# First products computed ahead of the feed-forward loop: for ten up sets of ten column pairs in place of the gate and up sets of five

## The chip, the cores and the metric

The kernel runs on one core of a Trainium2 chip. Its metric is the time of one execution in device microseconds (us). The kernel before took 1977.85 us as the median of three runs (1973.35 to 1978.29).

## The reference, cut to what matters

One decoder layer over 520 tokens (512 of a prompt, 8 samples, and 16 meta tokens that end before this stage). After attention and pooling come two layer norms with a feed-forward block between them. The change lies at the first of these two norms and in the gate and up products behind it:

```
h1 = layer_norm(DEEPNORM_ALPHA * h + mix, ln1_g, ln1_b)
a = jax.nn.silu(jnp.einsum('btd,df->btf', h1, w_gate)) * jnp.einsum('btd,df->btf', h1, w_up)
ff = jnp.einsum('btf,fd->btd', a, w_down)
return layer_norm(DEEPNORM_ALPHA * h1 + ff, ln2_g, ln2_b)
```

`h1` has 2048 columns, `w_gate` and `w_up` are 2048 x 5632, all in fp32.

## The kernel before, in words

**Tiling.** The 5632 hidden columns are 44 tiles of 128, taken as 22 column pairs (tile i and tile i + 22). For each pair there is one `Set` for the gate weights and one for the up weights (class at L924). A set multiplies a 2 x 2 block of weights by a 2 x 2 block of activations with seven products in place of eight (Winograd's form of Strassen's scheme): products 1 to 7, `Set.prod` at L941. The two halves of the tokens are 260 columns each, `HN`.

**One product.** Its weight block is 128 x 1024 fp32, in two halves of 512. Each half is split (L181) into a high part, a cast on ScalarE (ACT, L185), and a low part, a subtraction on VectorE (DVE, L186); then TensorE (PE) runs 12 matmuls on it (L201, L202, L204), so 24 for a product. The split halves live in a ring of five buffers (`WB`). Products 7, 6, 5 and 3 need a sum or difference of weight blocks first, made in place on VectorE by `weight_sum` (L191; it is recorded under L194). The sum for 7 overwrites block (1,0) from (0,0) and (1,0); for 6 it overwrites (1,0) from (1,1) and (1,0); for 5 it overwrites (0,0) from (1,0) and (0,0); for 3 it overwrites (0,1) from (0,1) and (1,0). So the sum for product 7 is the first sum of a set, and it wants blocks (0,0) and (1,0) in place; the sum for product 3 is the last reader of (1,0), and the splits of product 5 are the last readers of (0,0).

**Loads.** `load_raw` (L175) brings a 512 KB weight block in through SP's DMA queue (the issue is L178) into a ring of five buffers (`NRAW`). A set loads four blocks, in the order in which `run` asks for them. A load must wait until the block five loads before it in the ring has had its last reader. SP's queue also carries the staging stores of 260 KB to `t_d` (L1057, L1064).

**A set that runs in full** asks for (0,0), (1,0), (1,1), (0,1). It computes product 1, copies it out on ScalarE (L985), then products 7, 6, 2, 5, 4, 3, with two more copies on ScalarE (L995, L1001).

**Products ahead.** While the second half's layer norm is computed, TensorE would have nothing to do. Half of the tokens is normalised by then, so product 1, whose activations are block (1,1) of that half, can already be computed: `Set.ahead` (L958) does it with plain fp32 matmuls (L963) straight from the loaded weights. For the first two sets, the gate and up set of pair 0 (`NKEEP`), products 1 and 2 stay in PSUM. For the next ten sets (`NFILL`) product 1 is copied to SBUF by ScalarE (L968) into the `fill` tiles. `step` (L158) writes these matmuls' order on TensorE by hand.

**A filled set**, one with its first product ahead, runs six products: 7, 6, 2, 5, 4, 3. In place of the three copies on ScalarE it adds the stored product on VectorE three times (L993, L999, L1015). It asks for its blocks in the order (1,0), (0,0), (1,1), (0,1), since product 7 now comes first.

**Around it.** `turn` lists the pairs; the loop at L1095 runs `gate_out` and then `up_out` for each, with the staging of the pair before (`staged`, L1041: sums, casts and stores to `t_d`) as side steps within the gate set. Pairs are numbered here in the order of `turn`, from 0. On VectorE, ScalarE, SP and, outside the steps, on TensorE a planner orders the instructions by its own estimates of costs; each engine then runs its list in order.

Of the kernel before, what the change touches and what calls it, by code (L numbers as in the profile page):

```python
# [37 lines left out]
NFILL = 10  # L38
NF = 5
NKEEP = 2  # L40
# [26 lines left out]
def hybrid_step(ctx, tc, xin, w_in, w_o, w_g, w_u, w_d, w_pool, par_d, cst_d, ident_d, ln2gb, kct_d, vc_d, hist_d,  # L67
# [746 lines left out]
    for h in range(2):  # L814
        for k2 in range(KT // 2):
            mh[h].append(slot(f"mh{h}_{k2}"))
            ml[h].append(slot(f"ml{h}_{k2}"))
            for kk in range(2):
                s = mixf[2 * k2 + kk][:, HALF[h]]
# [255 lines left out]
    sets = [Set(w, i, f"{n}{i}") for i in turn for n, w in (("g", w_g), ("u", w_u))]  # L1075
    g1 = ln1(1, zs1)
    fills = [s.ahead(n) for n in (1, 2) for s in sets[:NKEEP]]
    for j, s in enumerate(sets[NKEEP:NKEEP + NFILL]):
        if j % 2 == 0:
            f = pb.tile([P, 2, HN], F32, tag="fill", name=f"fill{j}", bufs=NF)  # L1080
        fills.append(s.ahead(1, f[:, j % 2, :]))
# [314 lines left out]
```

## Time and profile before

| | |
|---|---|
| median of three runs | 1977.85 us (1973.35 to 1978.29) |
| the profiled execution's own time | 1976.38 us |
| its span, first to last instruction | 1974.6 us |
| TensorE busy | 1916.5 us, 97% |
| VectorE busy | 1545.2 us, 78% |
| ScalarE busy | 936.6 us, 47% |
| mean granted TensorE clock | 0.987 |

A busy share is an average over stages. In the gate and up stage (602 to 1490 us) the reader should look at single pairs: how long a pair takes, how many matmuls fall into it, and which wait ended last before an engine went on. A matmul's own duration (0.28 us) is longer than its distance from the next one, since matmuls overlap; counts of matmuls in a stretch tell more than busy time.

### The profile page before, as it was taken

What the parts mean: (1) busy time and instruction counts of PE and PEld (TensorE: products, weight loads), DVE (VectorE), ACT (ScalarE), POOL (GpSimd) and SP (SyncE); (2) the same over time, 40 slices, a digit from 0 to 9 for tenths busy, and PEclk for the clock granted to TensorE, in tenths of its full rate; (3) what the DMA queues carried; (4) which work ended last, traced back from release to release, by engine and by line L of the source; (5) the groups of instructions that cost most, each with busy time, mean ns of one, the idle gap of its engine ahead of it and who ended that gap; (6) DMA issues with size and microseconds to landing.
All of it is one profiled execution on the core that took longest, in us unless ns stands there. A gap on an engine that the chain in (4) does not pass through costs nothing.

```text
span 1974.6 us, 39350 instructions
## 1 busy us (share of the span) xinstructions
PE 1916.5 (97%) x15571; PEld 1881.8 (95%) x15571; DVE 1545.2 (78%) x2730; ACT 936.6 (47%) x1805; POOL 2.5 (0%) x8
## 2 busy tenths in 40 slices
PE   8999999999999999999999999999999999999995
PEld 8999999999988888999999999999999999999995
DVE  6665657766776878788888888888777888888878
ACT  6644445545654434455554545555545434344331
POOL 0000000000000000000000000000000000000000
PEclk9999999999999999999999999999999999999997
DMA  8732222665744453545445453545549664645332
GB/s 264 231 101 67 67 81 71 216 201 170 247 151 145 136 174 125 171 136 167 145 140 162 148 169 125 169 143 169 176 173 365 209 223 166 223 168 202 86 97 87
DMA packets 144984, 319.25 MB, mean 162 GB/s; under 512 B 14160, under 2 KB 65944, under 8 KB 144696
## 3 DMA queue, kind: packets, MB, share of 16 engines
q1 hardware_dynamic: 143680, 314.65, 48.2%
q8 instruction: 122, 2.00, 0.4%
q10 hardware_dynamic: 1120, 2.10, 0.3%
q14 instruction: 62, 0.51, 0.1%
HBM read 265.20 MB, written 54.03 MB: 162 GB/s over the span
## 4 chain that ended last, share of the span: by engine, by line
PE 58%; DVE 5%; DMA 2%; issue 1%; ACT 1%; DVEq 0%; ACTq 0%; SPq 0%
PE tri L201 7%; PE tri L204 7%; PE tri L202 7%; PE p_u L201 6%; PE p_u L202 6%; PE p_u L204 6%; PE p_g L201 6%; PE p_g L204 6%; PE p_g L202 6%; DMA fr<-in_w_g_dram 2%; DVE fr L194 2%; DVE rr L186 1%; PE d L204 1%; DMA t_d<-fr 1%; PE d L202 1%
## 5 line engine op out<-in xcount | busy, mean ns | idle before, releaser
L185 ACT CAST rr<-fr 128x512 fp32r<-128x512 f32 (+1 forms) x1056 | 655.6, 643 | 849.7 <-DVE fr L194 289.0
L186 DVE TENSOR_TENSOR rr<-fr,rr 128x512 fp32r<-128x512 f32 (+1 forms) x1056 | 733.4, 716 | 265.6 <-ACT rr L185 253.7
L194 DVE TENSOR_TENSOR fr<-fr 128x1024 f32<-128x1024 f32 (+1 forms) x304 | 319.3, 1050 | 37.3 <-DMA fr<-in_w_g_dram 21.7
L201 PE MATMUL p_g<-rr 128*128 128x260 f32 x800 | 231.2, 290 | 15.9 <-DVE fr L999 6.7
L204 PE MATMUL p_g<-rr 128*128 128x260 f32 x800 | 225.8, 287 | 1.1 <-DVE rr L186 1.1
L201 PE MATMUL p_u<-rr 128*128 128x260 f32 x800 | 225.5, 283 | 0.0
L204 PE MATMUL p_u<-rr 128*128 128x260 f32 x800 | 222.0, 282 | 0.0
L202 PE MATMUL p_g<-rr 128*128 128x260 f32 x768 | 219.6, 287 | 0.0
L202 PE MATMUL p_u<-rr 128*128 128x260 f32 x768 | 216.0, 282 | 0.0
L204 PE MATMUL tri<-rr 128*128 128x260 f32 x696 | 196.8, 283 | 1.2 <-DVE rr L186 1.2
L201 PE MATMUL tri<-rr 128*128 128x260 f32 x696 | 197.1, 283 | 0.8 <-ACT rr L185 0.8
L202 PE MATMUL tri<-rr 128*128 128x260 f32 x696 | 196.7, 283 | 0.0
L201 PEld LDWEIGHTS p_g<-rr 128*128 128x128 f32 x800 | 154.2, 193 | 19.9 <-DVE fr L999 7.7
L204 PEld LDWEIGHTS p_g<-rr 128*128 128x128 f32 x800 | 153.3, 193 | 1.4 <-DVE rr L186 1.3
L201 PEld LDWEIGHTS p_u<-rr 128*128 128x128 f32 x800 | 150.6, 188 | 0.0
L204 PEld LDWEIGHTS p_u<-rr 128*128 128x128 f32 x800 | 149.7, 189 | 0.0
L202 PEld LDWEIGHTS p_g<-rr 128*128 128x128 f32 x768 | 148.0, 193 | 0.0
L201 PE MATMUL o<-rr 128*128 128x260 f32 x512 | 146.0, 286 | 0.3 <-ACT rr L185 0.3
L202 PEld LDWEIGHTS p_u<-rr 128*128 128x128 f32 x768 | 144.3, 188 | 0.0
L204 PE MATMUL o<-rr 128*128 128x260 f32 x512 | 143.9, 283 | 0.2 <-DVE rr L186 0.2
L202 PE MATMUL o<-rr 128*128 128x260 f32 x512 | 144.0, 282 | 0.0
L204 PEld LDWEIGHTS tri<-rr 128*128 128x128 f32 x696 | 131.3, 189 | 1.7 <-DVE rr L186 1.4
(299 smaller groups left out, 4591.5 us busy)
## 6 DMA issues: line engine op xcount, KB each, us to landing
fr<-in_w_g_dram SPq DMA_DIRECT2D x95, 512.0 KB
fr<-in_w_u_dram SPq DMA_DIRECT2D x95, 512.0 KB
fr<-in_w_d_dram SPq DMA_DIRECT2D x64, 640.0 KB
t_d<-fr SPq DMA_DIRECT2D x140, 260.0 KB
fr<-in_w_o_dram SPq DMA_DIRECT2D x64, 512.0 KB
fr<-in_w_in_dram SPq DMA_DIRECT2D x46, 512.0 KB
rr<-t_d SPq DMA_DIRECT2D x87, 260.0 KB
mid_b<-t_d SPq DMA_DIRECT2D x53, 260.0 KB
```

The lines of the kernel that those rows point to most:

```text
L185: nc.scalar.copy(wh, s)
L186: last_lo[0] = (lo or nc.vector).tensor_sub(wl, s, wh.bitcast(F32)).ins
L194: i = op(*args).ins
L201: nc.tensor.matmul(o, wh, hi[j], start=first, stop=False, skip_group_check=onto)
L202: nc.tensor.matmul(o, wh, lo[j], start=False, stop=False, skip_group_check=onto)
L204: nc.tensor.matmul(o, wl, hi[j], start=False, stop=last, skip_group_check=onto)
```

## The change

One line changes, the choice of the ten sets whose product 1 is computed ahead:

```diff
     fills = [s.ahead(n) for n in (1, 2) for s in sets[:NKEEP]]
-    for j, s in enumerate(sets[NKEEP:NKEEP + NFILL]):
+    for j, s in enumerate(sets[NKEEP + 1::2][:NFILL]):
         if j % 2 == 0:
             f = pb.tile([P, 2, HN], F32, tag="fill", name=f"fill{j}", bufs=NF)
         fills.append(s.ahead(1, f[:, j % 2, :]))
```

`sets` alternates gate and up. Before, `sets[2:12]` are the gate and up sets of pairs 1 to 5. After, `sets[3::2][:10]` are the up sets of pairs 1 to 10. So the gate sets of pairs 1 to 5 run in full, and the up sets of pairs 6 to 10 become filled ones. The code of a set, which isn't changed, then goes one way or the other:

```python
            if not filled:
                self.p1 = r[:, HALF[0]]
                if al is None:
                    al = bank(f"p1_{self.name}")
                    self.prod(1, al)
                nc.scalar.copy(self.p1, al)
            else:
                al = bank(f"p1_{self.name}")
            ga = bank(f"p7_{self.name}")
            next(side, None)
            self.prod(7, ga)
```

## Rows read from the trace of the kernel before

**Rows 1.** The page: the span, and the busy time, share and instructions of each engine.

```profile
span 1974.6 us, 39350 instructions
PE 1916.5 (97%) x15571; PEld 1881.8 (95%) x15571; DVE 1545.2 (78%) x2730; ACT 936.6 (47%) x1805; POOL 2.5 (0%) x8
```

**Rows 2.** Busy time by stretch, one row for each of the pairs 1 to 10: stretch and its length in us, busy us (and instructions) of TensorE's matmuls, its weight loads, VectorE, ScalarE and GpSimd, then the granted TensorE clock, the DMA share and GB/s. A stretch begins where the up set of the pair before does its last multiplication on VectorE.

```profile
637.10:682.30 45.20, 40.71 (x326) 39.46 (x327) 38.03 (x63) 19.86 (x37) 0.00 (x0) 1.00 0.44 147
682.30:723.60 41.30, 37.53 (x290) 36.28 (x289) 33.35 (x56) 16.99 (x31) 0.00 (x0) 0.96 0.46 148
723.60:764.80 41.20, 37.45 (x290) 36.40 (x290) 33.45 (x57) 17.22 (x32) 0.00 (x0) 0.96 0.46 148
764.80:805.70 40.90, 37.65 (x290) 36.40 (x289) 33.31 (x56) 17.13 (x31) 0.00 (x0) 0.96 0.47 149
805.70:844.60 38.90, 36.90 (x293) 36.49 (x292) 32.24 (x55) 16.95 (x31) 0.00 (x0) 0.96 0.46 151
844.60:882.60 38.00, 36.66 (x301) 36.03 (x301) 32.54 (x53) 20.26 (x39) 0.00 (x0) 1.00 0.47 153
882.60:922.80 40.20, 40.20 (x338) 40.20 (x337) 34.30 (x54) 21.41 (x41) 0.00 (x0) 1.00 0.47 152
922.80:963.10 40.30, 40.30 (x338) 40.30 (x338) 34.34 (x54) 21.07 (x41) 0.00 (x0) 1.00 0.45 152
963.10:1003.40 40.30, 40.30 (x338) 40.30 (x337) 34.39 (x54) 21.21 (x41) 0.00 (x0) 1.00 0.45 151
1003.40:1043.70 40.30, 40.30 (x338) 40.30 (x337) 34.39 (x54) 21.43 (x41) 0.00 (x0) 1.00 0.48 152
```

**Rows 3.** Who waited for whom: what TensorE waited for from 640 to 885 us, and what VectorE's weight sums waited for from 640 to 850 us (us in total, times, longest).

```profile
PE p_g L201 <- ACT rr L185: 7.4, 10, 1.7
PE p_g L201 <- DVE fr L999: 6.7, 5, 1.4
...
DVE fr L194 <- DMA fr<-in_w_g_dram: 16.2, 5, 4.1
```

**Rows 4.** The chain of waits that ended last, 660 to 845 us, its five waits for a load of gate weights: start (the issue), us from there to the landing.

```profile
668.29 6.03 DMA fr<-in_w_g_dram
...
709.86 5.85 DMA fr<-in_w_g_dram
...
750.13 6.79 DMA fr<-in_w_g_dram
...
791.96 5.90 DMA fr<-in_w_g_dram
...
832.22 6.88 DMA fr<-in_w_g_dram
```

**Rows 5.** VectorE in order of time, from the filled up set of pair 5 through pair 6 (both sets in full): start, us, line, shape, count, and in brackets the idle time before it and what ended it. L194 is a weight sum, L186 the low part of a split.

```profile
820.00 1.28 DVE L186 TENSOR_TENSOR rr<-fr,rr 128x512 fp32r<-128x512 f32 x2
...
830.98 1.22 DVE L194 TENSOR_TENSOR fr<-fr 128x1024 f32<-128x1024 f32 x1
...
839.13 1.23 DVE L194 TENSOR_TENSOR fr<-fr 128x1024 f32<-128x1024 f32 x1 [2.33 <-DMA fr<-in_w_g_dram]
...
852.95 1.88 DVE L186 TENSOR_TENSOR rr<-fr,rr 128x512 fp32r<-128x512 f32 x3
...
860.01 1.23 DVE L194 TENSOR_TENSOR fr<-fr 128x1024 f32<-128x1024 f32 x1 [0.92 <-DMA fr<-in_w_u_dram]
...
861.98 1.29 DVE L186 TENSOR_TENSOR rr<-fr,rr 128x512 fp32r<-128x512 f32 x2 [0.41 <-ACT rr L185]
```

**Rows 6.** The same for single instructions elsewhere: the first weight sum of pair 1's gate set; in pair 8 the first sum of the up set with the splits behind it; the first sum of pair 9's and of pair 11's gate set.

```profile
634.47 1.23 DVE L194 TENSOR_TENSOR fr<-fr 128x1024 f32<-128x1024 f32 x1 [0.36 <-DMA fr<-in_w_g_dram]
...
940.91 1.22 DVE L194 TENSOR_TENSOR fr<-fr 128x1024 f32<-128x1024 f32 x1 [1.24 <-DMA fr<-in_w_u_dram]
...
942.87 1.29 DVE L186 TENSOR_TENSOR rr<-fr,rr 128x512 fp32r<-128x512 f32 x2 [0.40 <-ACT rr L185]
...
959.72 1.22 DVE L194 TENSOR_TENSOR fr<-fr 128x1024 f32<-128x1024 f32 x1
...
1040.30 1.22 DVE L194 TENSOR_TENSOR fr<-fr 128x1024 f32<-128x1024 f32 x1
```

**Rows 7.** SP's queue in order of time: loads issued behind the sums and splits that free their buffers, in the up set of pair 5 and in the gate sets of pairs 6 and 8 (x2 and x3: so many issues in a row, from that start).

```profile
829.28 3.27 SPq L178 DMA_DIRECT2D fr<-in_w_g_dram  x3
...
854.26 0.95 SPq L178 DMA_DIRECT2D fr<-in_w_u_dram  x2
...
934.24 0.95 SPq L178 DMA_DIRECT2D fr<-in_w_u_dram  x2
```

**Rows 8.** TensorE in order of time: the first matmul of the up set of pair 6 and of pair 8.

```profile
861.92 0.28 PE L201 MATMUL p_u<-rr 128*128 128x260 f32 x1
...
942.50 0.28 PE L201 MATMUL p_u<-rr 128*128 128x260 f32 x1
```

**Rows 9.** Groups of instructions by line, shapes apart: busy us in all, mean ns of one, idle time before them.

```profile
L186 DVE TENSOR_TENSOR rr<-fr,rr 128x512 fp32r<-128x512 f32 x264 | 174.0, 686 | 37.0 <-ACT rr L185 36.1 <-PE p_u L204 0.4
L1006 DVE TENSOR_TENSOR fr<-p_u,fr 128x260 f32<-128x260 f32 x10 | 4.2, 421 | 0.0
...
L963 PE MATMUL p_g<-fr 128*128 128x260 f32 x112 | 25.9, 382 | 0.0
L963 PE MATMUL p_u<-fr 128*128 128x260 f32 x112 | 25.7, 382 | 0.0
```

## The prediction, made before the changed kernel was run

> **What bounds the kernel now.** I read the page first. TensorE is busy 97% of the span, VectorE 78% [rows 1], so the whole kernel looks bound by TensorE. The second view, busy time by pair, says where that isn't so [rows 2]. Pairs 7 to 10, with all sets run in full, take 40.3 us for 338 matmuls and TensorE never pauses: 40.3 / 338 = 0.1192 us a matmul. Pairs 2 to 4, with both sets filled, have 48 matmuls fewer and still take about as long, 40.9 to 41.3 us. At 0.1192 a matmul the losses of pairs 1 to 6 (length less instructions times 0.1192) are 6.3, 6.7, 6.6, 6.3, 4.0 and 2.1, together 32.1 us. So the ten products ahead buy nothing here: TensorE saves 5.7 us a pair and then waits longer than that. The granted clock is a part of these losses: a mean of 0.96 in pairs 2 to 5, that is 2.4 GHz with some time at 1.2 GHz after TensorE's waits, and 1.00 behind.
>
> Third, who waited for whom [rows 3]: TensorE waits for splits on ScalarE and for VectorE's add at L999, and VectorE in turn for loads of gate weights, 16.2 us in five waits. Fourth, the chain of waits has these five loads with 5.85 to 6.88 us from issue to landing [rows 4]. So in filled pairs a loop of VectorE's work and loads sets the pace, not TensorE: the load is issued when the last reader of an older block in the ring of five is done, it lands six us later, and only then can VectorE's next sum begin. The question is how long this loop is after the change.
>
> **What the change removes and adds.** Five gate sets (pairs 1 to 5) go from filled to full, five up sets (pairs 6 to 10) the other way. A full set has one product more: two casts, two subtractions of 0.69 us, 24 matmuls and three copies on ScalarE, where a filled set has three adds of 0.42 us on VectorE [rows 9]. Five such trades in each direction: the sum over the kernel is zero on every engine. The ten products ahead are the same matmuls, 0.38 us each for both kinds of weights [rows 9], of the same 512 KB loads, at the same place: no cost and no gain, hidden or not. What moves is the pair's balance: pairs 1 to 10 each have one full gate set and one filled up set, 312 matmuls, 312 x 0.1192 = 37.2 us of TensorE. VectorE's work of a pair is about that of pairs 7 to 10, 34.3 us [rows 2].
>
> **The new loop, step by step.** In which buffers of the ring the blocks fall follows from five buffers and four loads a set. A full gate set loads (0,0), (1,0), (1,1), (0,1), the filled up set behind it (1,0), (0,0), (1,1), (0,1). Five loads back from the up set's (0,0) is the gate's (0,0), whose last reader is the split for product 5. Five loads back from the next gate's (1,0) is the up set's (1,0), whose last reader is the sum for product 3. Both loads are wanted by the first sum of their set. VectorE takes its list in order, so while that sum waits, nothing behind it starts: the splits of product 7, and with them all that TensorE is to get.
>
> Four terms make the loop.
> - A: from the first sum of a gate set to the issue of the up set's (0,0). The trace has this very transition, a full gate set behind a filled up set, in pair 6: the sum begins at 839.13 [rows 5], the load goes out at 854.26 [rows 7]: 15.13 us.
> - B: that load's landing. In pair 6 the next sum starts at 860.01, 5.75 us from the issue; in pair 8 at 940.91, from 934.24, 6.67 us [rows 5 to 7]. In both VectorE was waiting for the load, so these are landings. I take 6.21, their mean.
> - C: the filled up set, from its first sum to the issue of the load that its sum for product 3 frees. From the sum to the first split 1.96 us (940.91 to 942.87) [rows 6]; from the first split to that issue, in the up set of pair 5, 820.00 to 832.22, 12.22 us [rows 4, 5]; less one add of the gate set (L1015), 0.42, which a full gate set doesn't have [rows 9]. 13.76 us.
> - D: the landing of the next gate's (1,0). It is the third load in a row behind a filled up set [rows 7], as the five of the chain are: their mean is 6.29 us [rows 4].
>
> A + B + C + D = 15.13 + 6.21 + 13.76 + 6.29 = 41.4 us, more than TensorE's 37.2. So each of the ten pairs takes about 41.4 us, and TensorE waits some 4 us in it: 0.75 at the up set, where it arrives at 861.92 [rows 8] and product 7's first split is over only at 861.98 + 0.69 [rows 5], the rest in the gate set, where pair 6 lost 2.1 us [rows 2]. Product 1 of the up set covered the first of these, and covers it no more.
>
> From the first sum of pair 1's gate set (634.47) to that of pair 11 (1040.30) the kernel before takes 405.8 us [rows 6]; after, 10 x 41.4 = 414. Up to 634.47 nothing differs, and from pair 11 on both run full sets. The difference is 8.2 us. On the profiled execution's own 1976.38 us that is 1984.6; the median of the runs shown lies 1.5 above that execution, so 1986. Ends: B from 5.75 to 6.67 and D from 5.85 to 6.88 give loops of 40.5 to 42.4, 1977 to 1996.
>
> At B and D a rule speaks for a better end. The Trainium skill, DMA: Bandwidth & Descriptors, section Anatomy of one DMA, gives a transfer (on its GpSimd path) some 2.0 us fixed and its bytes at 436 GB/s. For 512 KB that is an estimate of 3.2 us, twice in the loop 6.4, and the loop would be 35.3 us, under TensorE's. The five waits of the chain show 5.85 to 6.88 us for such a load with others in the queue [rows 4], and by them the sum goes.
>
> **Rivals.** *TensorE sets the pace after all.* If A shrinks, as the planner may put pair 6's staging steps and multiplications behind the splits of product 5, or the landings are short, the loop falls under 38 us. It decides below 37.2: then ten pairs take 372 us, 34 less, 1944; with 3 us out of the loop, 38.4, it is 384, 22 less, 1956. For it: pairs 7 to 10 run without a pause at 85% of VectorE. Against: their planned order has been repeated in every pair, and pair 6, the only pair of the needed kind, lost time. The figure of the Trainium skill for a transfer (DMA: Bandwidth & Descriptors, Anatomy of one DMA) would lead here too.
>
> *It evens out.* With the landings at their low ends the loop is 40.5 us, hardly other than 40.6, the mean before (405.8 / 10): 1977 to 1980. For it: the third load's spread is wide [rows 4]. Against: in that case both landings must be low in all pairs.
>
> *Worse.* Each load shares SP's queue with the staging stores; at the high ends, 6.67 and 6.88, and with 0.5 us of a store's issue ahead of each, the loop is 43.4: 434 us, 28 more, 2006. It decides from 42.5 on. For it: landings of 6.79 and 6.88 stand in two of five waits. Against: they aren't the mean. A clock that falls in each pair, as in pairs 2 to 5, costs little by itself while VectorE's loop is the longer one: TensorE has 4 us to spare in it.
>
> **How the numbers follow.** 0.3% is 5.9 us, about what a measurement of this kernel can tell from no change. Chances: the loop of 41.4 and its neighbourhood (1979 to 1996) 0.52, of which 0.38 lies over 5.9 and 0.14 within; evening out 0.23, all within; TensorE's pace 0.17, all faster; worse 0.08. So faster 0.17, same 0.37, slower 0.46. The likeliest case's own range is 1977 to 1996. The range that should hold the time 8 times in 10 leaves out the ends of the two outer rivals: 1960 to 1996.
>
> **What would show it.** In the trace of the changed kernel: the first sum of a gate set recurs every 41.4 us in pairs 1 to 10; VectorE idles before it (2 to 3 us) for gate weights and before the up set's first sum (3 us) for up weights; L999 no longer holds TensorE in gate sets; the stretch of each of the ten pairs has about 314 matmuls and 41 us. TensorE without a pause in pairs 2 to 10 and sums 37 to 38 us apart would prove the first rival. If the sum of the up set stands at some other place in VectorE's order, or if (0,0) goes out before the split of product 5, the terms A and C are wrong and with them the sign.

## The result, and the profile after

The kernel after takes 1959.08 us (median of six runs, 1956.14 to 1960.61), beside 1975.98 us for six runs of the kernel before. The ratio is 0.9915, with a 95% interval of 0.9904 to 0.9927: faster by 0.85%. The forecast was 1986 us, slower, with a range of 1960 to 1996; the direction is wrong, and the time lies just below the range. The execution whose profile follows took 1960.28 us.

First the page of the kernel after (span, then busy time and instructions by engine), to be held against [rows 1]:

```profile
span 1958.5 us, 39300 instructions
PE 1909.2 (97%) x15571; PEld 1875.7 (96%) x15571; DVE 1542.9 (79%) x2730; ACT 937.9 (48%) x1805; POOL 2.5 (0%) x8
```

Every engine has as many of these instructions as before (the total of the first line also counts waits and issues), so the work is the same. The span is 16.1 us shorter. TensorE is busy for 7.3 us less, so 8.8 us of its waiting went, and 7.3 us in which the same matmuls ran more slowly.

Where it went, the second view says: busy time by pair of the kernel after, pairs 1 to 11, columns as in [rows 2] (the tenth row is pair 10, the last with a filled set).

```profile
636.40:678.10 41.70, 40.10 (x328) 39.27 (x327) 35.73 (x58) 19.51 (x37) 0.00 (x0) 1.00 0.46 154
678.10:717.50 39.40, 38.15 (x314) 37.53 (x313) 33.54 (x55) 19.31 (x36) 0.00 (x0) 1.00 0.46 155
717.50:755.60 38.10, 37.81 (x315) 37.52 (x314) 33.59 (x55) 19.31 (x36) 0.00 (x0) 1.00 0.48 160
755.60:794.90 39.30, 38.29 (x315) 37.67 (x314) 33.67 (x56) 19.31 (x36) 0.00 (x0) 1.00 0.47 156
794.90:832.80 37.90, 37.62 (x314) 37.41 (x313) 33.55 (x55) 19.30 (x36) 0.00 (x0) 1.00 0.47 161
832.80:871.30 38.50, 37.99 (x314) 37.57 (x314) 33.60 (x55) 19.30 (x36) 0.00 (x0) 1.00 0.49 159
871.30:911.00 39.70, 38.19 (x314) 37.57 (x313) 33.60 (x56) 19.30 (x36) 0.00 (x0) 1.00 0.47 154
911.00:950.50 39.50, 38.21 (x314) 37.58 (x313) 33.59 (x56) 19.30 (x36) 0.00 (x0) 1.00 0.47 155
950.50:989.60 39.10, 38.20 (x314) 37.57 (x313) 33.59 (x56) 19.30 (x36) 0.00 (x0) 1.00 0.47 156
989.60:1029.60 40.00, 38.17 (x314) 37.55 (x313) 33.56 (x56) 19.30 (x36) 0.00 (x0) 1.00 0.45 152
1029.60:1067.80 38.20, 38.20 (x320) 38.20 (x319) 32.57 (x52) 21.34 (x41) 0.00 (x0) 1.00 0.47 151
```

Pairs 1 to 10 together last 393.2 us and have 3156 matmuls. At 0.1192 us each these would be 376.2, so 17.0 us are lost: 10.5 in which TensorE isn't busy (393.2 less the 382.73 of the busy column), and 6.5 in which matmuls follow each other more slowly. The same sums over pairs 1 to 6 of [rows 2] give 18.6 and 13.5, the 32.1 us of the prediction. The loss was halved: 8.1 us of pauses went and 7.0 of slow matmuls. The granted clock is 1.00 in every row, where four rows of before have 0.96. The missing 0.04 of those four rows' 162.3 us is 6.5 us, about all of the slow matmuls that went.

Who still waits, in the kernel after from 640 to 1030 us (us in total, times, longest), beside [rows 3]:

```profile
PE p_u L201 <- ACT rr L185: 5.8, 7, 1.3
PE p_u L201 <- DVE fr L999: 2.9, 10, 0.3
PE p_u L204 <- DVE rr L186: 1.8, 8, 0.2
...
DVE fr L194 <- DMA fr<-in_w_u_dram: 34.4, 10, 4.3
```

All of TensorE's waits are now in the up sets (`p_u`), none in the gate sets. VectorE's weight sums wait for up weights, once in each of ten pairs, and no longer for gate weights. VectorE can afford most of that: of its 34.4 us TensorE's pauses show no more than the 10.5 that the three rows add up to, 5.8 of them for the casts behind such a sum.

VectorE in order of time, pair 4 of the kernel after: the first sum of the gate set, of the up set, then the sums for products 6, 5 and 3 of the up set, and the first sum of pair 5's gate set (columns as in [rows 5]).

```profile
750.15 1.22 DVE L194 TENSOR_TENSOR fr<-fr 128x1024 f32<-128x1024 f32 x1
...
771.88 1.22 DVE L194 TENSOR_TENSOR fr<-fr 128x1024 f32<-128x1024 f32 x1 [3.53 <-DMA fr<-in_w_u_dram]
...
775.19 1.22 DVE L194 TENSOR_TENSOR fr<-fr 128x1024 f32<-128x1024 f32 x1
...
778.91 1.22 DVE L194 TENSOR_TENSOR fr<-fr 128x1024 f32<-128x1024 f32 x1
...
780.99 1.22 DVE L194 TENSOR_TENSOR fr<-fr 128x1024 f32<-128x1024 f32 x1
...
789.37 1.22 DVE L194 TENSOR_TENSOR fr<-fr 128x1024 f32<-128x1024 f32 x1
```

And SP's queue there: the issue of the up set's (0,0) in pair 4, and that of the next gate set's (1,0).

```profile
765.56 0.35 SPq L178 DMA_DIRECT2D fr<-in_w_u_dram  x1
...
782.27 0.33 SPq L178 DMA_DIRECT2D fr<-in_w_g_dram  x1
```

The four terms of the forecast can be read here. A: 750.15 to 765.56, 15.41 us (forecast 15.13). B: 765.56 to 771.88, 6.32; the mean over the ten pairs is 6.23 (forecast 6.21). C: 771.88 to 782.27, 10.39, not 13.76. D: the load of 782.27 lands 3.84 us later (by its semaphore in the trace), first of its three and not third, and the gate set's sum at 789.37 doesn't wait for it. Gate sets' first sums stand 39.0 us apart on average (633.78 in pair 1 to 1024.11 in pair 11, ten pairs), not 41.4.

C is short because of VectorE's list. In the filled up sets of the kernel before, the planner put all four splits of products 5 and 4 ahead of the sum for product 3. After the change it puts one split of product 4 and then that sum straight behind the sum for product 5: 778.91 to 780.99 in the rows above. That sum frees the buffer of (1,0).

### The profile page after: what moved, and what is told of

Same layout as the page of the kernel before. It is cut to its first block, busy times and chain, and to the rows that moved or that the text cites. A ratio compares the mean times of both kernels' runs of the same rounds, so it can differ in the third digit from the quotient of the medians.

```text
span 1958.5 us, 39300 instructions
## 1 busy us (share of the span) xinstructions
PE 1909.2 (97%) x15571; PEld 1875.7 (96%) x15571; DVE 1542.9 (79%) x2730; ACT 937.9 (48%) x1805; POOL 2.5 (0%) x8
## 5 line engine op out<-in xcount | busy, mean ns | idle before, releaser
L186 DVE TENSOR_TENSOR rr<-fr,rr 128x512 fp32r<-128x512 f32 (+1 forms) x1056 | 733.1, 715 | 246.1 <-ACT rr L185 234.2
L194 DVE TENSOR_TENSOR fr<-fr 128x1024 f32<-128x1024 f32 (+1 forms) x304 | 319.3, 1050 | 50.9 <-DMA fr<-in_w_u_dram 44.4
L201 PE MATMUL p_g<-rr 128*128 128x260 f32 x830 | 233.9, 283 | 2.2 <-DVE fr L1009 2.2
L204 PE MATMUL p_g<-rr 128*128 128x260 f32 x830 | 230.8, 282 | 0.0
L201 PE MATMUL p_u<-rr 128*128 128x260 f32 x770 | 218.4, 284 | 2.9 <-DVE fr L999 2.9
L202 PE MATMUL p_g<-rr 128*128 128x260 f32 x788 | 221.2, 282 | 0.0
L204 PE MATMUL p_u<-rr 128*128 128x260 f32 x770 | 213.6, 282 | 0.0
L202 PE MATMUL p_u<-rr 128*128 128x260 f32 x748 | 210.7, 282 | 0.0
L201 PEld LDWEIGHTS p_u<-rr 128*128 128x128 f32 x770 | 144.9, 188 | 5.0 <-DVE fr L999 5.0
L204 PEld LDWEIGHTS p_u<-rr 128*128 128x128 f32 x770 | 143.9, 189 | 0.0
L202 PEld LDWEIGHTS p_u<-rr 128*128 128x128 f32 x748 | 140.6, 188 | 0.0
```

Source lines behind the costliest of these rows:

```text
L186: last_lo[0] = (lo or nc.vector).tensor_sub(wl, s, wh.bitcast(F32)).ins
L194: i = op(*args).ins
L201: nc.tensor.matmul(o, wh, hi[j], start=first, stop=False, skip_group_check=onto)
L202: nc.tensor.matmul(o, wh, lo[j], start=False, stop=False, skip_group_check=onto)
L204: nc.tensor.matmul(o, wl, hi[j], start=False, stop=last, skip_group_check=onto)
```

## The experiments

### Was it the place of one sum?

My first theory was this order: an early sum for product 3, so an early load, so no wait at the gate set. The rival said that loads don't matter and one filled set in each pair merely balances VectorE's work. A second rival was the clock, whose falls went. `e1_late_sum` puts the splits back in front of the sum, by chaining the low parts of a filled up set one behind the other (the sum is chained to the last of them in any case, L191):

```diff
...
-            last_lo[0] = (lo or nc.vector).tensor_sub(wl, s, wh.bitcast(F32)).ins
+            prev, last_lo[0] = last_lo[0], (lo or nc.vector).tensor_sub(wl, s, wh.bitcast(F32)).ins
+            if chain[0]: tc.add_manual_dep(last_lo[0], prev.name, mybir.DependencyInfo(mybir.DependencyClass.NoSync, mybir.DependencyReason.DATA), reason="low")
...
+            chain[0] = filled and self.name[0] == "u"
             self.prod(5, al, False)
...
```

> The changed kernel, with one thing put back: in the filled up sets VectorE does the four splits of products 5 and 4 ahead of the sum for product 3, as it did in the up sets of the kernel before. No work is added. Order theory (the early sum lets the next gate set's (1,0) be asked for 3.4 us sooner and first in line, and that is what my forecast missed): the loop of my forecast closes again, 40.5 to 41.4 us a pair for 39.0, 15 to 24 us more, 1974 to 1983; the gate set's first sum waits for its weights again. Balance theory (one filled set in each pair evens out VectorE's work, and loads don't matter): no change, 1959. Clock theory (the gain is the falls of the granted clock that went): no change, 1959, unless falls come back without other losses.

Measured: 1956.94 us, ratio to before 0.9897 (0.9884 to 0.9911). My theory fell: the late sum that I had forecast with costs nothing. VectorE in order of time in this run (the sums are recorded under L195 here), the first sums of gate and up set of pair 2, and of pair 10's up set and pair 11's gate set:

```profile
671.39 1.22 DVE L195 TENSOR_TENSOR fr<-fr 128x1024 f32<-128x1024 f32 x1 [1.20 <-DMA fr<-in_w_g_dram]
...
691.27 1.23 DVE L195 TENSOR_TENSOR fr<-fr 128x1024 f32<-128x1024 f32 x1 [2.41 <-DMA fr<-in_w_u_dram]
...
1001.44 1.23 DVE L195 TENSOR_TENSOR fr<-fr 128x1024 f32<-128x1024 f32 x1 [3.22 <-DMA fr<-in_w_u_dram]
...
1019.60 1.23 DVE L195 TENSOR_TENSOR fr<-fr 128x1024 f32<-128x1024 f32 x1 [1.15 <-DMA fr<-in_w_g_dram]
```

The loop of the forecast does close here: both first sums wait for their loads in every pair. But it is shorter than forecast. From 671.39 to 1019.60 are nine pairs of 38.69 us. Its terms, as means of these nine, are A 14.41, B 5.80, C 13.05 and D 5.43, 38.69 together, 2.7 less than 41.4.

The reverse, `e3_before_early`, gives the kernel before the early sum in its filled up sets:

```diff
...
+            if filled and self.name[0] == "u":
+                p5 = self.s((0, 0), (1, 0), (0, 0), nc.vector.tensor_add)
+                w4 = split(self.q(1, 1)[:, 512:1024], f"{self.name}_41")
+                self.pre = {5: p5, (4, 1): w4, 3: self.s((0, 1), (0, 1), (1, 0), nc.vector.tensor_sub)}
             self.prod(5, al, False)
```

> The kernel before, with its choice of sets, and one thing taken from the changed kernel: in the filled up sets VectorE does the second split of product 4 and the sum for product 3 ahead of the splits of product 5. No work is added or taken away. Order theory: the gate set's load of (1,0) goes out some 3 us sooner in pairs 1 to 5 and lands sooner; pairs 1 to 5 fall from 40.6 to 38 to 39 us, 1962 to 1968. Balance theory: no change, 1976. Clock theory: 1976 less what falls of the clock go, at most 9.

Measured: 1974.64 us, ratio 0.9995 (0.9986 to 1.0004), no change. What VectorE waited for from 640 to 815 us in this run:

```profile
DVE rr L186 <- ACT rr L185: 12.5, 16, 2.1
DVE fr L1016 <- PE p_u L204: 8.8, 4, 2.2
```

No wait for a load is left, and pairs 3 to 5 still take 41.3, 39.7 and 41.3 us:

```profile
714.20:755.50 41.30, 37.70 (x290) 36.45 (x289) 33.41 (x56) 17.71 (x32) 0.00 (x0) 0.96 0.46 148
755.50:795.20 39.70, 36.10 (x290) 34.84 (x289) 33.24 (x55) 17.41 (x32) 0.00 (x0) 1.00 0.48 154
795.20:836.50 41.30, 37.66 (x291) 36.41 (x290) 36.14 (x58) 18.93 (x35) 0.00 (x0) 0.96 0.46 146
```

(In these rows, and in the stretches of all later runs but `e2_gate_fills`, a stretch begins one multiplication earlier, at what is L1033 in the kernel before, as the planner moves the last one about. By it pair 1 of the kernel before takes 40.4 us, and pairs 2 to 5 take 40.9 to 41.3.)

But the planner answered the edit with another list: the gate set's first sum now stands behind adds that wait for TensorE's products. The edit exchanged one wait for another, so this run doesn't decide about loads. It does say something of the clock: VectorE has the same list in pairs 3 and 4, the clock fell in pair 3 and not in pair 4, and pair 4 is 1.6 us shorter, all of it in TensorE's busy time. So falls of the clock can lengthen a pair, and the four in the kernel before may have cost it as much as 6 of the 17 us. No run changed the clock alone, so this share stays open.

### Is it the up sets, or one filled set in each pair?

`e2_gate_fills` takes `sets[NKEEP::2][:NFILL]`, the ten gate sets.

> Ten filled sets in ten pairs as in the changed kernel, but the gate sets instead of the up sets. Balance theory: as the changed kernel, 1957 to 1962. Order theory: the up sets are full and have their sum for product 3 late, as full up sets always do here, so a gate set's first sum can wait for weights again: 1962 to 1975. If it matters that side steps of the staging fall into full sets (they run during gate sets), a filled gate set has more adds beside them: slower than the changed kernel too.

Measured: 1957.69 us, 0.9903 (0.989 to 0.9917), as the kernel after. A pair of it, by stretch:

```profile
718.70:757.00 38.30, 37.65 (x314) 37.44 (x313) 33.77 (x55) 19.49 (x37) 0.00 (x0) 1.00 0.49 159
```

VectorE waits for no load in pairs 2 to 5; TensorE loses some 0.7 us in each to the add at L999. So it hardly matters which of the two sets is filled, as the rival with the balance said; its other half, that loads don't matter, falls with the sixth buffer below.

### The wait that is left in the kernel after

The load of the up set's (0,0) takes the buffer of the gate set's (0,0), free at the split for product 5. If the gate set asks for (1,0) first, the up set's (0,0) takes the buffer of (1,0), free at the sum for product 3. `e9_after_q10` does only this; `e10_after_early` only writes the early order of the up sets out, with the lines of `e3_before_early`; `e5_q10_early` does both.

```diff
...
             filled = self.p1 is not None
+            if self.name[0] == "g" and not filled and self.bk.get(1) is None:
+                self.q(1, 0)
...
```

> The changed kernel, with the full gate set of each of the pairs asking for (1,0) ahead of (0,0), so that the up set's (0,0) takes the buffer that the gate set's early sum for product 3 frees and not the one that its split for product 5 frees; the early order of the filled up sets is written out. Order theory (what is left, some 1.4 us a pair at the up sets, is the wait of the up set's first sum for its (0,0)): that load goes out 1.8 us sooner and first in line, the waits at up sets go, 1946 to 1952. Balance theory and clock theory: no change, 1959. If the gate set's own (0,0), now tied to the up set's sum for product 3, lands too late for product 1, the gain is given back there: 1955 to 1965.

> The changed kernel with the early order of its filled up sets written out, as in the run that also asked for (1,0) first, but without that: the gate sets ask for (0,0) first, as in the changed kernel. Load theory (the up set's (0,0) still waits for the gate set's split for product 5): the up set's first sum waits as in the changed kernel, pairs of 38.5 to 39.3 us, 1955 to 1960. If the written-out order was what helped there: pairs of 37.4 to 37.8, 1944 to 1949.

> The changed kernel with only the full gate set of each of the pairs asking for (1,0) ahead of (0,0); nothing of VectorE's order is written out. Load theory: the up set's first sum no longer waits, pairs of 37.4 to 37.8 us and 1944 to 1949, as with the written-out order. If the early sum in the up sets was what helped there, the pairs in which the sum comes late stay at 38.5 us or more: 1950 to 1956.

Measured: both 1945.70 us, 0.9841 (0.9827 to 0.9854); the order alone 1961.34, 0.9933 (0.9917 to 0.9948); the load's place alone 1956.21, 0.9898 (0.9881 to 0.9914). Weight sums that waited for up weights, from 673 to 1020 us, first with the order alone and then with both, and a pair with both:

```profile
DVE fr L194 <- DMA fr<-in_w_u_dram: 25.5, 9, 4.1
```

```profile
DVE fr L194 <- DMA fr<-in_w_u_dram: 1.5, 2, 1.0
```

```profile
751.30:788.70 37.40, 37.40 (x315) 37.40 (x314) 33.41 (x56) 19.58 (x36) 0.00 (x0) 1.00 0.51 163
```

Between `e10_after_early` and `e5_q10_early` lie two lines, and they are worth 15.6 us, together with what the planner made of them: its lists differ too, and the order alone has two that alternate. In pair 4 the load goes out 12.08 us after the gate set's first sum (15.41 in the kernel after) and lands in 3.92 us, being first in line; no sum waits, and TensorE runs without a pause at its own 37.4 us a pair. That was expected; the order alone came 1.3 us above what was expected of it. The load's place without the written-out order missed its expectation: the sums wait no more (0.6 us of load waits in pairs 2 to 5), but the planner's list then alternates, and every second pair loses about 2 us in the gate set, to casts and low parts that come late. Both together are the fastest version found, 13.4 us below the kernel after.

### One buffer more

If a ring of five buffers is what sets the pace, a sixth must take the loss away with either choice of sets. With six products ahead there is room for it (the same lines for either choice):

```diff
-NFILL = 10
-NF = 5
+NFILL = 6
+NF = 3
...
+    wp.rings["raw"][0].append((fr, fr.take(1024)))
...
```

> The choice of sets of the kernel before, with a sixth buffer in the ring of raw weight blocks from the second stage on. The room comes from four products ahead fewer: pairs 1 to 3 have both sets filled, all others run in full, so the pairs are compared and not the time. Load theory (in the kernel before the loop of VectorE and weight loads sets the pace of such a pair): VectorE's waits for weights go and pairs 2 and 3 fall from 41.3 us to 35 to 38 us, TensorE's own need being 34.3. Hand-off theory (TensorE, ScalarE and VectorE wait for each other in filled sets, as the kernel before with the early sum suggests, where VectorE no longer waited for any load and the pairs still took 41 us): 40 to 41.5 us.

> The choice of sets of the changed kernel, with a sixth buffer in the ring of raw weight blocks from the second stage on, paid for with four products ahead: pairs 1 to 6 have a full gate set and a filled up set, all others run in full, so the pairs are compared and not the time. Load theory (what TensorE still loses in such a pair is the up set's first sum waiting for its weights): pairs 2 to 6 fall from 39.0 us to 37.4 to 37.7. Balance theory (loads don't matter): 38.5 to 39.5 us.

Each ran once: 1950.71 us with the choice of before, 1948.83 with that of after. Pairs 2 and 3 took 36.4 and 35.0 us in the first, pairs 2 to 6 each 37.43 in the second. But the control of the first, `e13_before_fill6`, with six products ahead and five buffers, was a warning.

> The control of the run with six buffers: the choice of sets of the kernel before, six products ahead (pairs 1 to 3 with both sets filled), five buffers. Load theory: pair 3 takes 40.5 to 41.5 us as in the kernel before, where it took 35.0 with six buffers; the whole comes at 1960 to 1968, some 15 us over the run with six buffers. If the smaller number of products ahead and not the buffer shortened the pairs there: 35 to 37 us here too, and 1950 to 1953.

Measured: 1956.68 us, 0.9918 (0.99 to 0.9935), with 36.0 and 38.1 us for pairs 2 and 3, between the two expectations. Three filled pairs may still live on blocks that were loaded ahead; no run shows that, but they are too few to show the pace of ten. A fourth staging buffer with eight products ahead (`NT = 4`, `NFILL = 8`, `NF = 4`), `e7_before_stage4`, tested the 8.2 us that VectorE waits in pairs 2 to 5 of the kernel before for a staging store to leave its buffer (L1062):

> The choice of sets of the kernel before, with four instead of three buffers for the staging tiles that are stored to device memory. The room comes from two products ahead fewer: pairs 1 to 4 have both sets filled, so the pairs are compared and not the time. Staging theory (in the kernel before VectorE waits 2 us in each up set for a staging store to leave its buffer, and that wait lengthens the loop): pairs 2 to 4 fall from 41.3 us to about 39. Load theory without it: the wait goes, the gate set's first sum waits for its weights as long as before or longer, 40.5 to 41.5 us.

One run, 1970.48 us: the staging wait is gone, pairs 3 and 4 take 41.4 and 40.2 us, and three sums wait 8.8 us for gate weights. So this wait isn't what made the pairs long.

So the sixth buffer had to come without giving up products ahead. The pairs need fewer row buffers than the layer norm, and from pair 0 on two of sixteen can be its place:

```diff
+    rows = ap_.rings["row"][0]
+    wp.rings["raw"][0].append((fr, rows[14][1]))
+    fr.give(rows[14][1] + 1024, 16)
+    del rows[14:]
+    ap_.rings["row"][2] = wp.rings["raw"][2] = 0
+    nraw[0], nrow[0] = 6, 14
     side = ()
...
```

> The kernel before with all of its ten products ahead, and a sixth buffer in the ring of raw weight blocks from pair 0 on, made of two of the sixteen row buffers, which the layer norm needs and the pairs don't. Load theory: all of pairs 1 to 5 come to 34.4 to 36.5 us, as with six products ahead, for 41 in the kernel before; some 25 us less, 1945 to 1952. If the head start and not the buffer made the pairs short there, pairs 3 to 5 take 38 to 41 us, 1962 to 1976.

> The changed kernel with the same sixth buffer in the place of two row buffers, all ten products ahead kept. Load theory: pairs 1 to 10 of 37.4 us, TensorE's own time, 1943 to 1948, and the same time as the kernel before with six buffers, since then it no longer matters which sets are filled. Otherwise 38.5 to 39.5 us a pair and 1955 to 1960.

> The choice of sets of the kernel before with eight products ahead (pairs 1 to 4 with both sets filled) and five buffers. The planner's list for VectorE in pairs 3 and 4 is here that of the runs with six buffers, not that of the kernel before. Load theory: five buffers give 38 to 41 us in pairs 3 and 4 with this list too, and VectorE waits for weights. Order theory (the list of the kernel before made it slow): 35 to 36.5 us.

Measured: the choice of before with six buffers 1953.85 us, 0.9883 (0.9864 to 0.9902); that of after with six 1948.66, 0.9857 (0.9839 to 0.9876); eight products ahead with five buffers 1956.04, 0.9894 (0.9877 to 0.991). By stretch, pairs 2 to 5 of the first, pair 2 of the second, and pairs 2 to 4 of the third with, from 700 to 781 us, what VectorE's sums waited for:

```profile
666.20:702.70 36.50, 35.72 (x298) 35.52 (x297) 34.47 (x58) 17.18 (x31) 0.00 (x0) 1.00 0.54 173
702.70:738.10 35.40, 34.81 (x291) 34.60 (x290) 32.87 (x56) 17.01 (x31) 0.00 (x0) 1.00 0.53 172
738.10:774.50 36.40, 35.14 (x291) 34.72 (x290) 33.01 (x57) 17.01 (x31) 0.00 (x0) 1.00 0.52 169
774.50:810.30 35.80, 34.54 (x286) 34.12 (x285) 32.03 (x55) 17.46 (x32) 0.00 (x0) 1.00 0.51 170
```

```profile
671.40:708.80 37.40, 37.40 (x314) 37.40 (x313) 33.82 (x54) 19.38 (x37) 0.00 (x0) 1.00 0.50 159
```

```profile
665.90:702.20 36.30, 35.12 (x284) 34.09 (x283) 34.59 (x58) 17.06 (x31) 0.00 (x0) 1.00 0.51 165
702.20:740.50 38.30, 35.70 (x291) 34.86 (x290) 33.26 (x57) 17.18 (x31) 0.00 (x0) 1.00 0.49 162
740.50:780.60 40.10, 36.30 (x286) 35.67 (x285) 32.40 (x56) 17.45 (x32) 0.00 (x0) 0.96 0.47 153
```

```profile
DVE fr L194 <- DMA fr<-in_w_u_dram: 5.3, 2, 3.2
```

With six buffers the filled pairs of before take 35.4 to 36.5 us, all five of them, near TensorE's 34.3; those of after take TensorE's 37.4. For the kernel after this settles it: with nearly the same list on VectorE, the sixth buffer takes away every wait of TensorE in pairs 1 to 10. For the choice of before it shows less, since VectorE's list changed with the buffer. `e16_before_fill8` has nearly the list of the run with six buffers in pairs 3 and 4, and with five its pairs lengthen, 36.3, 38.3, 40.1, as up weights come late. Pairs 2 to 4 together take 123.5 us in the kernel before, 114.7 in `e16_before_fill8` and 108.2 with six buffers. The buffer is worth the last 6.5 of these (a fall of the clock in pair 4 among them). What of the other 8.8 is the list, the smaller number of products ahead or the clock, no run shows. The times of the two choices didn't come out equal, as I had expected: 5.2 us lie between them, and they are 1.9 and 0.7 us above what was expected of each. Some 6 are what pairs 1 to 5 still lose to L999 and to casts in the choice of before. The Trainium skill names this pattern (Perfetto Trace Analysis, section Optimization Strategy): the same gap again and again, on an engine that should be full, can mean too few buffers. These runs agree: nothing is lost in pairs 1 to 10 of the kernel after with six buffers, where 17.0 us were with five.

### What the products ahead are worth, and the queue

`e11_no_fills` sets `NFILL` to 0.

> No products ahead for the ten further sets at all (those of the first pair stay), so all pairs from 1 on run in full. Load theory: full pairs are TensorE's, 40.3 us, where the kernel before takes 40.6 with ten products saved; so the products ahead bought the kernel before nothing and cost it what they take at the layer norm. Four products ahead more move the end of pair 0 from 628 to 635 us in the runs with six and ten, about 1.6 each; without any it would come at 619 to 628, and the whole at 1950 to 1960. If the products ahead are free at the layer norm: 635 and the whole at 1968 to 1974.

Measured: 1962.03 us, 0.9936 (0.992 to 0.9951). Pair 3 by stretch:

```profile
708.40:748.70 40.30, 40.30 (x339) 40.30 (x338) 34.34 (x54) 21.08 (x42) 0.00 (x0) 1.00 0.43 141
```

So the ten products ahead cost the kernel before 14 us. In the profiled executions pair 11 begins 11 us earlier without them, and most of that lies ahead of pair 1; the pairs take 40.3 us each, the first ten of the kernel before 40.6 on average. So it paid for the products at the layer norm and got nothing back in the pairs. The time lies between the two expectations, 2 us above the first. After the change they bring some 3 us (1959.1 beside 1962.0, intervals that just overlap), and with the load's place and order put right 16.

`e12_after_store_queue` issues the staging stores from GpSimd (`nc.gpsimd.dma_start(t_d...` for `nc.sync`).

> The changed kernel with the staging stores of the pairs issued by GpSimd, not by SyncE, so that no weight load stands behind a store in SyncE's queue. The bytes are the same. If a load's landing is long because of the stores ahead of it in its queue: (0,0) lands in 4 to 5 us for 6.2, the up set's wait shrinks by 1.2 to 2, pairs of 37.4 to 38 us, 1946 to 1951. If the landing is long because of the other loads and of the transfers' common engines: no change, pairs of 39.0, 1956 to 1960.

Measured: 1961.90 us, 0.9936 (0.9916 to 0.9956). In pairs 2 to 10 (0,0) lands in 5.73 us for 6.08, and the pairs take 38.7 us for 39.1; the span of its profiled execution is that of the kernel after, 1958.5 us, since pair 2 begins 3.8 us later there. Two falls of the clock, at 616.7 and 661.1, stand in front of it, which the kernel after doesn't have, so the time isn't a clean measure of the edit. The landing is: a store ahead in the queue is at most a small part of a long one. The Trainium skill says as much (DMA: Bandwidth & Descriptors, section Issuing engines are not separate DMA queues): another issuing engine saves the time of the issue, while the transfers share the same DMA engines.

## Why the prediction was wrong

- *What bounds the kernel*: right in the main. A sixth buffer takes the loss away with either choice of sets. For the kernel after that is shown with nearly the same list on VectorE; in the kernel before VectorE's list and the falls of the clock have a share that no run parts from it, and `e3_before_early` shows that its pairs stay as long when waits for TensorE stand in the place of those for loads.
- *No work is added or removed*: right. The counts of [rows 1] are the same, and the first sum of pair 1's gate set comes at 633.78 for 634.47 [rows 6].
- *A and B*: right in the kernel after, 15.41 and 6.23 us for 15.13 and 6.21.
- *C and D*: here it failed. Both were read in the up set of pair 5 of the kernel before [rows 4, 5] and carried into pairs of another make. In the kernel after C is 10.39 for 13.76, as the planner ordered VectorE's list anew, and D isn't on the path at all: the gate set's sum waits for no load. So the loop as I drew it doesn't close. What remains is A + B, and then 17.5 us from the up set's first sum to the next gate set's (771.88 to 789.37), in which TensorE runs through: it pauses only at the up set, until its (0,0) is there and split, and loses 1.7 us a pair on average (17.0 / 10).
- *The sum, 41.4 us*: it would have been wrong even with the order I assumed. With it put back all four terms came out shorter than forecast, by 0.72, 0.41, 0.71 and 0.86, so 38.69. Each was off by 5 to 14%, all to the same side, and the sum is taken ten times: 2.7 x 10 = 27 us of the 29 between 1986 and the 1956.94 of that run. The signs of the errors weren't independent, and my low end, 40.5 a pair, only let B and D vary.
- *The rivals*: "TensorE sets the pace after all" comes closest. It is right that the loop falls short of what I added up, and that the end of a pair is then TensorE's. It isn't right on the place: A didn't shrink but grew a little, and at 39.0 us the pairs lie between its condition (below 37.2) and the forecast. What I held against it, that pair 6 lost time, was weak: pair 6 is the end of the filled pairs, and inherits their delay.
- *The clock*: I put it as a part of the loss, and it is. In pairs 1 to 6 of before 13.5 us were slow matmuls, in pairs 1 to 10 of after 6.5. That the falls go when TensorE's waits get shorter, I hadn't counted as a gain. I wrote that a fall costs little while VectorE's loop is the longer one; the two pairs of `e3_before_early` with the same list show 1.6 us for one, where VectorE waits for TensorE and not for loads.
- *What would show it*: "if the sum stands at some other place in VectorE's order, A and C are wrong and with them the sign" named the right sign, but for the wrong sum, and `e1_late_sum` shows that the place of the sum for product 3 wasn't what decided the sign.

Why A and C were 0.7 us too long, the rows of VectorE say. First three of the kernel before (the gate set's add at L1012 in the up set of pair 5, the last staging subtraction of pair 6's gate set, the same add in the up set of pair 8), then two of `e1_late_sum` in pair 4 (its staging subtraction is L1065):

```profile
821.20 0.42 DVE L1012 TENSOR_TENSOR fr<-fr,p_g 128x260 f32<-128x260 f32 x1
...
852.34 0.69 DVE L1062 TENSOR_TENSOR fr<-fr 128x520 fp32r<-128x520 f32 x1
...
942.05 0.42 DVE L1012 TENSOR_TENSOR fr<-fr,p_g 128x260 f32<-128x260 f32 x1
```

```profile
762.00 1.28 DVE L186 TENSOR_TENSOR rr<-fr,rr 128x512 fp32r<-128x512 f32 x2
763.20 0.69 DVE L1065 TENSOR_TENSOR fr<-fr 128x520 fp32r<-128x520 f32 x1
```

In pair 6 of before the subtraction stands ahead of the splits for product 5 (852.95 in [rows 5]), whose second frees the buffer; in `e1_late_sum` it stands behind them. That is A's 0.7. C counted the add at L1012 twice: it lies between the sum and the first split in pair 8, and again in the stretch of pair 5, from which only L1015 was taken off. And in that stretch VectorE waits 1.0 us for casts, in `e1_late_sum` 0.35. These two are about 1 us together; small differences the other way leave C's 0.7. Still open is what of B and D is due to which other transfer: no run took these apart.

## What to carry to other kernels

When a loop sets the pace, measure it as a whole in the surroundings in which it will run; four terms read elsewhere and added can all be off to one side, and the repeat count multiplies it. Look for the resource that closes the loop, here a ring of five buffers, and ask which reader frees which buffer: changing the order of two loads was worth 15.6 us where VectorE's order was written out, about as much as the change itself, and 2.9 where the planner was left free to answer it. And price a saving against none at all: ten products saved on TensorE cost the kernel 14 us as long as TensorE wasn't what set the pace.

## What the runs showed of the hardware

- The same 512 KB load lands in 3.7 to 4.1 us when it is first in line (the ten gate blocks (1,0) of the kernel after; 3.84 above) and in 5 to 7 when it follows another one within 2 us (4.97 to 7.03 for (0,0) in the kernel after). The prediction's estimate of 3.2 us, from the Trainium skill's DMA: Bandwidth & Descriptors, section Anatomy of one DMA, fits neither; it comes near the first.
- The granted clock fell to 1.2 GHz (0.50 in the rows) at 772.0 in pair 4 of before, after TensorE had waited 0.59 and 1.41 us shortly before, and at 763.1 in pair 4 of `e16_before_fill8`, the row with 0.96, after a wait of 2.8 us. It didn't in pairs 1 to 10 of the kernel after, where the longest wait was 1.3 us. The waits alone don't decide it: pairs 3 and 4 of `e3_before_early` have the same three (1.1, 0.59 and 1.0 us), and the clock fell in the first alone. That one fall made the pair 1.6 us longer.
